# The last token block's closing step of an encoder kernel, with a fixed order on TensorE and its results on three engines

## The chip, the core and the metric

The kernel runs on one core of a Trainium2 chip. The metric is device time in microseconds (us): the median of three executions. One more execution was taken by the hardware profiler; its rows are quoted here. The engines are TensorE (PE, matmuls and transposes), VectorE (DVE), ScalarE (ACT), GpSimd (POOL) and SyncE (SP, which issues the DMAs here). PE reads operands from SBUF and writes PSUM; DVE and ACT read both; POOL adds from SBUF to SBUF here.

## What is computed

One step of a one-layer streaming encoder on 1,024 prompt tokens and 32 sample tokens of width 1,024: a feed-forward part, two attention mixers, and a second feed-forward part. The change lies in the last lines of the layer:

```
h = adaln_in(x, gains[4], sh3, sc3)
x = x + FFN_RES * g3[:, None] * rmsnorm(swiglu(h, w2_gate, w2_up, w2_down), gains[5])

def swiglu(h, w_gate, w_up, w_down):
    return (jax.nn.silu(h @ w_gate) * (h @ w_up)) @ w_down
```

`rmsnorm` divides by the root of the mean square over the 1,024 features (plus a small constant) and multiplies by a gain. All of it is float32.

## The kernel before

Tokens are cut into three blocks of 384, 384 and 288 tokens (`TB`, L27); block 2 holds two tiles of 128 prompt tokens and one of the 32 sample tokens. Inside the kernel an activation is kept with features on the partitions: eight tiles of 128 features (`KT`), tokens along the free dimension. The output wants tokens on the rows, so in the end every 128x128 piece is turned on PE (`te.transpose`).

`ffn` (L525) runs the second feed-forward part in groups of two of the 22 slices of the hidden width. For each block `up` makes gate and up products (48 matmuls each slice in `mm3`, three a product) and `down` multiplies with the down weights into a two-bank PSUM tile `dn` for each pair of feature tiles and adds it into `facc` on DVE (L581), four accumulations a block. In the last group `down` also steps the block's closing step, `finale` (L1297), once after each accumulation, and afterwards leaves it in the list `side`, whose pieces are handed out by `step` between other work and run to the end by `finish` (L488).

`finale` of a block: squares of `facc` on ACT (L364), added up on POOL for the first two pairs of features and on DVE for the others (L368, L370), one matmul set with a vector of ones that sums over the partitions (`pss`, L357; three token tiles, six PE records), a reciprocal root on DVE (L330 to L339, ten small steps on a 128x3 tile), the scaling of `facc` by gate and gain on ACT (L1304) and DVE (L1306) in turn, the turns of `facc` on PE (`py`, L1313: four a piece), and for each piece one DVE instruction (L1315) that multiplies the turned piece by the token's root and adds the residual: `xp <- py * y + xp`. Below, such an instruction is called a result. There are two results to a token tile, and one output DMA to each tile (L1318).

The residual comes from `xs_dram` with features on the partitions as well. `tokens_first` (L1282) loads it (`raw`, L1288), turns it on PE (`px`, L1293) and copies it to `xp` on ACT (L1294). For block 2 it is begun beside the last slice of block 1.

PSUM is held in three pools: `ps2` has two tiles of two banks (`dn`), `ps1` three of one bank (`gate`, `up`, `px`, `py`), `psc` one (`pss`). The order on each engine is made when the kernel is built, by a list scheduler that goes by a model of the times; inside a `manual_schedule` block the named engine keeps the order of the code. In SBUF the tags `u`, `h` and `r` are rings of six, five and three buffers (`xp`; `sq`; `raw`).

Of the kernel before, what the change touches and what calls it, by code (L numbers as in the profile page):

```python
# [7 lines left out]
F32 = mybir.dt.float32  # L8
F32R = mybir.dt.float32r
I32 = mybir.dt.int32  # L10
AF = mybir.ActivationFunctionType
OP = mybir.AluOpType
# [4 lines left out]
D = 1024  # L17
KT = D // 128
DFF = 2816
NF = DFF // 128  # L20
SEQ = 1024
# [5 lines left out]
TB = [(0, 384), (384, 384), (768, 288)]  # L27
SEGS = [[(0, 384, 0)], [(0, 384, 0)], [(0, 256, 0), (256, 288, 1)]]
# [46 lines left out]
def encoder_step(ctx: ExitStack, tc, x_prompt, x_sample, cache_a_k, cache_a_v, cache_b_k, cache_b_v,  # L75
# [27 lines left out]
    def h_tile(shape, name, dt=F32):  # L103
        return hpool.tile(shape, dt, name=name, tag="h")
# [4 lines left out]
    def p2(name, shape=(128, 2, 512)):  # L109
        return ps2.tile(list(shape), F32, name=name, tag="p2")  # L110

    def pc(name, shape=(128, 512)):
        return psc.tile(list(shape), F32, name=name, tag="pc")

    def p1(name, shape=(128, 512)):
        return ps1.tile(list(shape), F32, name=name, tag="p1")
# [225 lines left out]
    def token_cols(w):  # L342
        return [(c, min(128, w - c)) for c in range(0, w, 128)]
# [126 lines left out]
    def token_tiles(tb):  # L470
        t0, w = TB[tb]
        return [(t0 + c, c, 128) for c in range(0, w - w % 128, 128)] + ([(SEQ, w - DEC, DEC)] if w % 128 else [])
# [4 lines left out]
    def step(n):  # L477
        for _ in range(n):
            while side:
                turn[0] += 1  # L480
                i = turn[0] % min(ABREAST, len(side))
                try:
                    next(side[i])
                    break
                except StopIteration:
                    side.pop(i)

    def finish():  # L488
        while side:
            step(1)  # L490
# [3 lines left out]
    def begin(key, gen, first=False):  # L494
        side.insert(0 if first else len(side), marked(key, gen))
# [29 lines left out]
    def ffn(key, H, F, wg, wu, wd, per_group, key_out, after, beside=lambda ff, tb: None):  # L525
        late, pre = [], {}
        plan = rounds(*ROUNDS[key])
        begun = set()
        final = {tb: max(i for i, (g, t) in enumerate(plan) if tb in t) for tb in range(3)}

        def load(r, ff):
            pre[r, ff] = (split_cols(wg, ff), split_cols(wu, ff))

        load(0, 0)
        yield
        for r, (gi, blocks) in enumerate(plan):
            grp = GROUPS[gi]
            wgu, wds, gs = {}, {}, {}

            def up(ff, tb):  # L540
                need((key, tb))
                w = TB[tb][1]
                hi, lo = H[tb]
                ps = [p1("gate"), p1("up")]
                for s in range(2):
                    for k in range(KT):
                        mm3(ps[s][:, :w], wgu[ff][s], k, hi[:, k, :], lo[:, k, :], k == 0, k == KT - 1)
                    step(FAST if gi == 0 else PACE)
                sl = s_tile([128, 384], "sl")
                ae.activation(sl[:, :w], ps[0][:, :w], AF.Silu)  # L550
                ve.tensor_tensor(sl[:, :w], sl[:, :w], ps[1][:, :w], op=OP.mult)  # L551
                g = g_tile([128, 2, 384], "gg", F32R)
                ae.activation(g[:, 0, :w], sl[:, :w], AF.Copy)
                ve.tensor_sub(g[:, 1, :w], sl[:, :w], g[:, 0, :w])  # L554
                gs[ff, tb] = g
                beside(ff, tb)
                if late:
                    late.pop()()

            def down(tb, r=r, grp=grp, wds=wds, gs=gs):  # L560
                w = TB[tb][1]
                new = tb not in begun
                begun.add(tb)
                if new:
                    F[tb] = u_tile(tb, "facc", F32)
                if r == final[tb]:
                    if key_out != "y" or tb == 0:
                        finish()
                    own = marked((key_out, tb), after(tb))
                for mp in range(KT // 2):  # L570
                    ps = p2("dn")
                    for s in range(2):
                        for i, ff in enumerate(grp):
                            g = gs[ff, tb]
                            mm3(ps[:, s, :w], wds[ff], 2 * mp + s, g[:, 0, :w], g[:, 1, :w],
                                i == 0, i == len(grp) - 1)
                    o = F[tb][:, 2 * mp:2 * mp + 2, :]
                    if new:
                        ve.tensor_copy(o, ps[:, :, :w])
                    else:  # L580
                        ve.tensor_tensor(o, ps[:, :, :w], o, op=OP.add)  # L581
                    if r == final[tb]:
                        next(own)
                    step(1)
                if r == final[tb]:
                    side.append(own)

            x, y = grp
            if r:
                load(r, x)  # L590
            load(r, y)
            if r == XAT and key == "h1":
                XIN[1] = load_x(1)
            wgu.update({x: pre[r, x], y: pre[r, y]})
            for ff in grp:
                wds[ff] = split_rows(wd, ff)
            for tb in blocks:
                up(x, tb)
                up(y, tb)
                if len(begun) < 2:  # L600
                    down(tb)
                else:
                    late.append(lambda down=down, tb=tb: down(tb))
            if (gi, 2) == (gi, blocks[-1]):
                per_group(gi)
        late.pop()()


# [669 lines left out]
    F3 = [None] * 3  # L1278

    XP = {}  # L1280

    def tokens_first(tb):  # L1282

        xp = upool.tile([128, 3, KT, 128], F32, name="xp", tag="u", bufs=6)
        for i, (t, c0, n) in enumerate(token_tiles(tb)):
            xt = XP[tb, i] = xp[:, i]
            xr = rpool.tile([128, KT, 128], F32, name="raw", tag="r")
            dma.dma_start(xr[:, :, :n], xs_dram[2][tb][:, :, c0:c0 + n])  # L1288
            yield
            for hf in range(2):  # L1290
                pt = p1("px", (128, 4, 128))
                for k in range(4):
                    te.transpose(pt[:n, k, :], xr[:, 4 * hf + k, :n], ident)  # L1293
                ae.activation(xt[:n, 4 * hf:4 * hf + 4], pt[:n], AF.Copy)  # L1294
                yield

    def finale(tb):  # L1297
# [10 lines left out]
        for i, (t, c0, n) in enumerate(token_tiles(tb)):  # L1308
# [9 lines left out]
            dma.dma_start(dst.rearrange("t (k c) -> t k c", c=128), xt[:n])  # L1318
            yield

    def beside(ff, tb):
        if ff == NF - 1 and tb < 2:
            for t in ((0, 1), (2,))[tb]:
                begin(("xp", t), tokens_first(t))

    for _ in ffn("h3", H3, F3, w2_gate, w2_up, w2_down, lambda gi: None, "y", finale, beside):
        pass
    finish()

# [26 lines left out]
```

## Time and profile before

| | us |
|---|---|
| median of 3 runs | 2213.52 |
| lowest and highest run | 2210.39, 2215.9 |
| profiled execution, own time | 2217.6 |
| its span (first to last instruction) | 2215.8 |
| PE busy | 2161.6 (98%) |
| DVE busy | 1239.1 (56%) |
| ACT busy | 697.8 (31%) |
| POOL busy | 179.2 (8%) |

Times in rows are us from the span's start. A timeline row has start, length, engine, line, operation, output<-inputs, shapes and, in brackets, the idle time before it with what ended it; "x2" merges neighbours. The granted clock is that of PE: 1.00 stands for 2.4 GHz and 0.50 for 1.2 GHz, and a value between is a stretch with some of both.

### The profile page before, as it was taken

To read this page: it belongs to the slowest core of one execution; us is meant where nothing else is said; L and a number is where in the kernel's file an instruction comes from. 1 tells how busy PE (TensorE), PEld (TensorE's weight loads), DVE (VectorE), ACT (ScalarE), POOL (GpSimd) and SP (SyncE) were. 2 spreads that over 40 slices of the span, in tenths; PEclk is the share of its full clock that TensorE was granted. 3 is DMA by queue.
4 is the path that set the end of the run, shared out by engine and by line. 5 is a ranking of instruction groups with operands and counts; after the bars stand their busy time and mean duration, and the time that the engine had idled before them with its cause. 6 is when DMAs were issued, how large, how long until landed. Compare 5 with 4: busy or idle time off the path is not lost.

```text
span 2215.8 us, 33976 instructions
## 1 busy us (share of the span) xinstructions
PE 2161.6 (98%) x14012; PEld 2068.6 (93%) x14012; DVE 1239.1 (56%) x2425; ACT 697.8 (31%) x1450; POOL 179.2 (8%) x281
## 2 busy tenths in 40 slices
PE   6999999999999999899999899999999999999998
PEld 4999999999999999799787589999999999999998
DVE  5788667874333497677444865785333333333336
ACT  4411111111121253576444663542111111111133
POOL 1100000000000023001110313220000000000000
PEclk8999999999999999899999899999999999999999
DMA  9253334434122352111112121424211111111122
GB/s 323 93 153 118 111 96 124 143 101 129 39 66 69 101 184 93 38 39 30 50 30 62 46 77 67 134 86 120 66 58 39 57 39 39 58 38 58 39 69 79
DMA packets 200623, 186.03 MB, mean 84 GB/s; under 512 B 7597, under 2 KB 169813, under 8 KB 199317
## 3 DMA queue, kind: packets, MB, share of 16 engines
q1 hardware_dynamic: 200468, 183.87, 27.1%
q8 instruction: 110, 1.80, 0.3%
q14 instruction: 45, 0.36, 0.1%
HBM read 164.12 MB, written 22.86 MB: 84 GB/s over the span
## 4 chain that ended last, share of the span: by engine, by line
PE 90%; DVE 4%; DMA 3%; ACT 1%; issue 1%; POOL 0%; SPq 0%; ACTq 0%; DVEq 0%; POOLq 0%
PE dn L325 7%; PE dn L326 7%; PE dn L327 7%; PE gate L327 7%; PE gate L326 7%; PE up L327 7%; PE up L326 7%; PE gate L325 7%; PE up L325 7%; PE po L713 3%; PE S L752 2%; PE pq L325 2%; PE pq L327 2%; PE pq L326 2%; DMA raw<-in_w_gate_dram 1%; PE pp L776 1%
## 5 line engine op out<-in xcount | busy, mean ns | idle before, releaser
L326 PE MATMUL gate<-h_lo,w 128*128 128x384 f32 (+1 forms) x1056 | 340.2, 322 | 4.0 <-DVE h_lo L446 4.0
L325 PE MATMUL dn<-gg,w 128*128 128x384 f32 (+1 forms) x1056 | 341.4, 325 | 1.1 <-DVE facc L581 1.0
L581 DVE TENSOR_TENSOR facc<-dn,facc 128x768 f32<-128x768 f32 (+1 forms) x240 | 212.9, 889 | 230.2 <-PE dn L327 229.9
L326 PE MATMUL dn<-gg,w 128*128 128x384 f32 (+1 forms) x1056 | 340.6, 323 | 0.6 <-DVE gg L554 0.6
L325 PE MATMUL gate<-h_hi,w 128*128 128x384 f32 (+1 forms) x1056 | 341.0, 323 | 0.0
L327 PE MATMUL gate<-h_hi,w 128*128 128x384 f32 (+1 forms) x1056 | 340.4, 322 | 0.0
L325 PE MATMUL up<-h_hi,w 128*128 128x384 f32 (+1 forms) x1056 | 340.2, 322 | 0.0
L326 PE MATMUL up<-h_lo,w 128*128 128x384 f32 (+1 forms) x1056 | 340.0, 322 | 0.0
L327 PE MATMUL dn<-gg,w 128*128 128x384 f32 (+1 forms) x1056 | 340.0, 322 | 0.0
L327 PE MATMUL up<-h_hi,w 128*128 128x384 f32 (+1 forms) x1056 | 339.9, 322 | 0.0
L304 DVE TENSOR_TENSOR w<-raw,w 128x1024 fp32r<-128x1024 f32 x187 | 231.5, 1246 | 150.5 <-ACT w L303 150.3
L303 ACT ACTIVATE w<-raw 128x1024 fp32r<-128x1024 f32 x187 | 195.7, 1056 | 266.1 <-PE dn L327 103.5
L550 ACT ACTIVATE sl<-gate 128x384 f32<-128x384 f32 (+1 forms) x132 | 60.9, 462 | 563.9 <-PE gate L327 560.9
L551 DVE TENSOR_TENSOR sl<-sl,up 128x384 f32<-128x384 f32 (+1 forms) x132 | 68.5, 519 | 292.1 <-PE up L327 286.1
L326 PEld LDWEIGHTS gate<-h_lo,w 128*128 128x128 f32 x1056 | 198.6, 188 | 4.6 <-DVE h_lo L446 4.6
L325 PEld LDWEIGHTS dn<-gg,w 128*128 128x128 f32 x1056 | 199.2, 189 | 1.6 <-DVE facc L581 1.2
L326 PEld LDWEIGHTS dn<-gg,w 128*128 128x128 f32 x1056 | 199.2, 189 | 1.0 <-DVE gg L554 0.9
L327 PEld LDWEIGHTS dn<-gg,w 128*128 128x128 f32 x1056 | 199.1, 189 | 0.0
L325 PEld LDWEIGHTS gate<-h_hi,w 128*128 128x128 f32 x1056 | 198.7, 188 | 0.1
L327 PEld LDWEIGHTS gate<-h_hi,w 128*128 128x128 f32 x1056 | 198.7, 188 | 0.0
L327 PEld LDWEIGHTS up<-h_hi,w 128*128 128x128 f32 x1056 | 198.7, 188 | 0.0
L325 PEld LDWEIGHTS up<-h_hi,w 128*128 128x128 f32 x1056 | 198.5, 188 | 0.0
(224 smaller groups left out, 3367.4 us busy)
## 6 DMA issues: line engine op xcount, KB each, us to landing
raw<-in_w_mod_dram SPq DMA_DIRECT2D x56, 512.0 KB, 4.0
raw<-in_w_gate_dram SPq DMA_DIRECT2D x54, 512.0 KB, 4.0
raw<-in_w_up_dram SPq DMA_DIRECT2D x54, 512.0 KB, 4.7
raw<-in_w_down_dram SPq DMA_DIRECT2D x54, 512.0 KB, 4.5
raw<-in_w_in_dram SPq DMA_DIRECT2D x18, 512.0 KB, 4.3
wm<-in_w_mod_dram SPq DMA_DIRECT2D x8, 1024.0 KB, 7.4
raw<-in_w_out_dram SPq DMA_DIRECT2D x13, 512.0 KB, 4.5
xr<-xs SPq DMA_DIRECT2D x16, 384.0 KB, 3.5
```

The source lines that it names most:

```text
L303: ae.activation(w[:, 0], r, AF.Copy)
L304: ve.tensor_sub(w[:, 1], r, w[:, 0])
L325: te.matmul(ps, w[:, 0, k], hi, start=start, stop=False)
L326: te.matmul(ps, w[:, 0, k], lo, start=False, stop=False)
L327: te.matmul(ps, w[:, 1, k], hi, start=False, stop=stop)
L550: ae.activation(sl[:, :w], ps[0][:, :w], AF.Silu)
L551: ve.tensor_tensor(sl[:, :w], sl[:, :w], ps[1][:, :w], op=OP.mult)
L581: ve.tensor_tensor(o, ps[:, :, :w], o, op=OP.add)
L713: te.matmul(po[64 * h:64 * h + 64, :n], vsl(j, h, kn), PT(h, j, kn), start=j == 0, stop=j == nt - 1)
L752: te.matmul(S[:, c:ce], self.T[:, h, :], KQ[:, 0, 128 * k0 + c:128 * k0 + ce], start=True, stop=True)
L776: te.transpose(pp[:, j - j0, :], P[:, 128 * j:128 * j + 128], ident)
```

## The change

`ffn` no longer steps `side` inside the last block's `down`, and it runs `finish` ahead of that `down`, so that what is left of the other blocks' closing steps stands before it in the code. Block 2 gets a closing step of its own, `finale_last`. Its residual is loaded beside its own last slice (`load_xr`) and turned only after the down-projection, in a fixed order on PE. The square sum is taken in three products (the folded sum of three pairs, and both halves of the last pair) instead of one. The results of the 32-token tile are a scaled copy on ACT and an add on POOL; the other four stay on DVE. Each half tile is stored by a DMA of its own.

```diff
-                    step(1)
+                    if key_out != "y" or tb < 2:
+                        step(1)
...
+        if key_out == "y":
+            finish()
         late.pop()()
...
+    def load_xr(tb, i):
+        t, c0, n = token_tiles(tb)[i]
+        xr = XR[tb, i] = rpool.tile([128, KT, 128], F32, name="raw", tag="r")
+        dma.dma_start(xr[:, :, :n], xs_dram[2][tb][:, :, c0:c0 + n])
+
+    def turn_x(xt, xr, n, hf):
+        pt = p1("px", (128, 4, 128))
+        for k in range(4):
+            te.transpose(pt[:n, k, :], xr[:, 4 * hf + k, :n], ident)
+        ae.activation(xt[:n, 4 * hf:4 * hf + 4], pt[:n], AF.Copy)
...
+    def finale_last():
+        f, tb = F3[2], 2
...
+        for c in range(KT // 2):
+            sq = h_tile([128, 2, 384], "sq")
+            ae.activation(sq[:, :, :w], f[:, 2 * c:2 * c + 2, :], AF.Square)
+            if c < 3:
+                e = ge if c < 2 else ve
+                e.tensor_tensor(sq[:, 0, :w], sq[:, 0, :w], sq[:, 1, :w], op=OP.add)
+                if acc is not None:
+                    e.tensor_tensor(sq[:, 0, :w], sq[:, 0, :w], acc[:, 0, :w], op=OP.add)
+                acc = sq
...
+            yield
+
+        def turn_f(pt, i, k0):
+            t, c0, n = toks[i]
+            for k in range(4):
+                te.transpose(pt[:n, k, :], f[:, k0 + k, c0:c0 + n], ident)
+            return pt[:n]
+
+        def residual(i, hf):
+            turn_x(xp[:, i], XR[tb, i], toks[i][2], hf)
+
+        with tc.manual_schedule(engines={mybir.EngineType.PE}):
+            pss = pc("pss")
+            for q, (part, h) in enumerate(((acc, 0), (sq, 0), (sq, 1))):
+                if q == 1:
+                    residual(0, 0)
+                    residual(0, 1)
+                    residual(2, 0)
+                for j, (c0, m) in enumerate(token_cols(w)):
+                    te.matmul(pss[:m, j:j + 1], part[:, h, c0:c0 + m], ones, start=q == 0 and j == 0, stop=q == 2,
+                              skip_group_check=True)
+            y = rstd_cols(pss, w, 1.0 / D)
+            pts = {}
+            for i in (0, 2, 1):
+                bank = p2("py2", (128, 2, 4, 128)) if i < 2 else None
+                for hf in range(2):
+                    if (i, hf) in ((2, 1), (1, 0), (1, 1)):
+                        residual(i, hf)
+                    pts[i, hf] = turn_f(p1("py", (128, 4, 128)) if bank is None else bank[:, hf], i, 4 * hf)
+        for i, hf in ((2, 0), (0, 0), (0, 1), (2, 1), (1, 0), (1, 1)):
+            t, c0, n = toks[i]
+            o, pt, yc = xp[:n, i, 4 * hf:4 * hf + 4], pts[i, hf], y[:n, i:i + 1]
+            if i == 2:
+                z = h_tile([128, 4, 128], "yz")
+                ae.activation(z[:n], pt, AF.Copy, scale=yc)
+                ge.tensor_tensor(o, z[:n], o, op=OP.add)
+            else:
+                ve.scalar_tensor_tensor(o, pt, yc, o, op0=OP.mult, op1=OP.add)
+            dst = y_sample[0] if t == SEQ else y_prompt[0, t:t + 128]
+            dma.dma_start(dst.rearrange("t (k c) -> t k c", c=128)[:, 4 * hf:4 * hf + 4], o)
```

`load_xr` is called for block 2 from `beside`, in the place where `begin(("xp", 2), ...)` was. The scaling of `facc` (L1352 and L1354 of the new code) stands in the lines left out and is as before.

The order on PE from the last down-projection matmuls on, before (`px` turns the residual, `py` the facc; the 28 turns are 24 of block 1 and the first four of block 2):

```order
L327 MATMUL dn<-gg,w 128x288
L1293 MATMUL px<-ident,raw 32x128 x4
L1313 MATMUL py<-ident,facc 128x128 x28
L357 MATMUL pss<-ones,sq 128x1 x2
L357 MATMUL pss<-ones,sq 32x1
L1313 MATMUL py<-ident,facc 128x128 x12
L1313 MATMUL py<-ident,facc 32x128 x8
```

And on PE from the same place in the changed kernel:

```order
L1374 MATMUL pss<-ones,sq 128x1 x2
L1374 MATMUL pss<-ones,sq 32x1
L1295 MATMUL px<-ident,raw 128x128 x8
L1295 MATMUL px<-ident,raw 32x128 x4
L1374 MATMUL pss<-ones,sq 128x1 x2
L1374 MATMUL pss<-ones,sq 32x1
L1374 MATMUL pss<-ones,sq 128x1 x2
L1374 MATMUL pss<-ones,sq 32x1
L1360 MATMUL py_20406<-ident,facc 128x128 x8
L1360 MATMUL py<-ident,facc 32x128 x4
L1295 MATMUL px<-ident,raw 32x128 x4
L1360 MATMUL py<-ident,facc 32x128 x4
```

Behind these come four residual turns, four of `facc`, and the same once more. The 24 turns of block 1 have moved up among the down-projection matmuls (four after the first six of them, then four and four, and twelve ahead of the last twelve matmuls), where 20 residual turns of block 2 stood.

On DVE, from block 2's third and fourth accumulation (L581) on, before (L1306 scales `facc`, L368 and L370 add squares, L1315 are block 1's results):

```order
L581 TENSOR_TENSOR facc<-dn,facc 128x576 x2
L368 TENSOR_TENSOR sq<-sq 128x288
L1306 TENSOR_SCALAR facc<-facc,gcoef 128x256
L1306 TENSOR_SCALAR facc<-facc,gcoef 128x32
L1315 SCALAR_TENSOR_TENSOR xp<-py,ry,xp 128x512
L370 TENSOR_TENSOR sq<-sq 128x288
L1315 SCALAR_TENSOR_TENSOR xp<-py,ry,xp 128x512
L368 TENSOR_TENSOR sq<-sq 128x288
L1306 TENSOR_SCALAR facc<-facc,gcoef 128x256
L1315 SCALAR_TENSOR_TENSOR xp<-py,ry,xp 128x512
```

Behind these rows a scaling step, the last add of squares and three more results stand ahead of the root. And on DVE from the last step of block 1's root on in the changed kernel:

```order
L338 SCALAR_TENSOR_TENSOR ry<-rt,ry 128x3
L1328 SCALAR_TENSOR_TENSOR xp<-py,ry,xp 128x512 x3
L581 TENSOR_TENSOR facc<-dn,facc 128x576
L1354 TENSOR_SCALAR facc<-facc,gcoef 128x256
L1354 TENSOR_SCALAR facc<-facc,gcoef 128x32
L581 TENSOR_TENSOR facc<-dn,facc 128x576
L1328 SCALAR_TENSOR_TENSOR xp<-py,ry,xp 128x512 x3
L1354 TENSOR_SCALAR facc<-facc,gcoef 128x256
L1354 TENSOR_SCALAR facc<-facc,gcoef 128x32
L581 TENSOR_TENSOR facc<-dn,facc 128x576
L1345 TENSOR_TENSOR sq<-sq 128x288
```

Then come a scaling pair, the second add of squares (L1347), a scaling pair and the root. Block 1's six results have moved ahead of the second and the fourth accumulation, and one pair of square adds is gone. On ACT the squares and scalings of block 2 now run without residual copies between them; the copies, two scaled copies (L1389) and the last two residual copies close the queue. On POOL two adds of 32x512 (L1390) follow the adds of squares. SP's order is the old one up to block 1's outputs; then come six half-tile outputs in the order of the tiles 0, 0, 2, 1, 2, 1.

## Rows read from the trace of the kernel before

**Rows 1.** Page: shares of the chain that ended last, by engine.

```profile
PE 90%; DVE 4%; DMA 3%; ACT 1%; issue 1%; POOL 0%; SPq 0%; ACTq 0%; DVEq 0%; POOLq 0%
```

**Rows 2.** Windows: length; busy PE, PEld, DVE, ACT, POOL; clock; DMA share; GB/s.

```profile
2199.00:2206.00 7.00, 5.00 (x40) 4.00 (x38) 6.91 (x16) 3.18 (x7) 0.00 (x0) 1.00 0.27 110
2206.00:2215.80 9.80, 3.75 (x20) 2.47 (x18) 6.23 (x19) 0.00 (x0) 0.00 (x0) 0.61 0.53 202
```

**Rows 3.** Timeline of DVE, from block 2's first accumulation to the end.

```profile
2193.42 0.76 DVE L581 TENSOR_TENSOR facc<-dn,facc 128x576 f32<-128x576 f32 x1 [0.32 <-PE dn L327]
...
2196.72 1.78 DVE L1306 TENSOR_SCALAR facc<-facc,gcoef 128x256 f32<-128x256 f32 x2 [0.65 <-ACT sq L364]
2198.41 1.41 DVE L581 TENSOR_TENSOR facc<-dn,facc 128x576 f32<-128x576 f32 x2
...
2200.29 0.50 DVE L1306 TENSOR_SCALAR facc<-facc,gcoef 128x256 f32<-128x256 f32 x2
2200.69 0.74 DVE L1315 SCALAR_TENSOR_TENSOR xp<-py,ry,xp 128x512 f32<-128x512 f32 x1
...
2204.47 0.46 DVE L370 TENSOR_TENSOR sq<-sq 128x288 f32<-128x288 f32 x1
...
2206.16 0.16 DVE L388 TENSOR_SCALAR rv<-pss 128x2 f32<-128x2 f32 x1
...
2208.36 4.47 DVE L1315 SCALAR_TENSOR_TENSOR xp<-py,ry,xp 128x512 f32<-128x512 f32 x6
```

**Rows 4.** Timeline of SP's queue: the last output DMA.

```profile
2212.86 0.33 SPq L1318 DMA_DIRECT2D out_dram<-xp  x1
```

**Rows 5.** Timeline of PE: the last matmul of the last down-projection.

```profile
2198.61 0.30 PE L327 MATMUL dn<-gg,w 128*128 128x288 f32 x1
```

**Rows 6.** Timeline: adds on POOL, and a DVE accumulation beside one of them.

```profile
2180.69 1.01 POOL L370 TENSOR_TENSOR sq<-sq 128x384 f32<-128x384 f32 x1
2180.75 0.94 DVE L581 TENSOR_TENSOR facc<-dn,facc 128x768 f32<-128x768 f32 x1
...
2196.76 0.81 POOL L368 TENSOR_TENSOR sq<-sq 128x288 f32<-128x288 f32 x1 [0.99 <-ACT sq L364]
```

**Rows 7.** Pieces of the chain: start, length, what, instructions merged.

```profile
2152.27 1.31 PE px L1293 x12
...
2190.56 0.56 PE pss L357 x6
...
2209.26 2.81 PE py L1313 x12
```

**Rows 8.** Timeline of PE: a slow product set, and three long waits.

```profile
26.22 1.44 PE L357 MATMUL pss<-ones,sq 128*128 128x1 f32 x6 [3.20 <-POOL sq L370]
...
920.53 0.39 PE L813 MATMUL Sb<-KSB,qs 128*128 128x256 f32 x1 [2.38 <-ACT Ps L888]
...
1442.92 0.45 PE L326 MATMUL gate<-h_lo,w 128*128 128x384 f32 x1 [2.13 <-DVE h_lo L446]
...
2209.26 2.79 PE L1313 MATMUL py<-ident,facc 128*128 128x128 f32 x12 [2.30 <-DVE xp L1315]
```

**Rows 9.** Windows of PE: length, busy (instructions), granted clock, DMA share, GB/s.

```profile
921.00:921.50 0.50, 0.50 (x5) 0.89 0.07 12
...
924.50:925.00 0.50, 0.50 (x4) 0.70 0.00 0
...
1443.40:1443.80 0.40, 0.40 (x3) 0.79 0.00 0
...
2208.00:2208.50 0.50, 0.00 (x0) 0.72 0.74 295
...
2209.50:2210.00 0.50, 0.50 (x4) 0.50 0.00 0
```

**Rows 10.** Timeline of ACT, one copy; line L467 on POOL: min/median/max ns, shapes.

```profile
2200.54 0.57 ACT L1294 ACTIVATE xp<-px 32x512 f32<-32x512 f32 x1
...
L467 POOL TENSOR_TENSOR facc<-facc,xr x6: 1432/1850/1855, 775.7 to 878.4; 128x768 f32<-128x768 f32 x4, 128x576 f32<-128x576 f32 x2
```

More of the change, by code (lines that the diff above doesn't have):

```diff
@@ L1280, in encoder_step @@
     XP = {}
+    XR = {}
+    def load_xr(tb, i):
[7 more added lines that the diff above has]
+        ae.activation(xt[:n, 4 * hf:4 * hf + 4], pt[:n], AF.Copy)
     def tokens_first(tb):
@@ L1286, in tokens_first @@
             xt = XP[tb, i] = xp[:, i]
-            xr = rpool.tile([128, KT, 128], F32, name="raw", tag="r")
-            dma.dma_start(xr[:, :, :n], xs_dram[2][tb][:, :, c0:c0 + n])
+            load_xr(tb, i)
             yield
+            xr = XR.pop((tb, i))
             for hf in range(2):
[L1291 to L1294, printed above, removed]
+                turn_x(xt, xr, n, hf)
                 yield
@@ L1319, in finale @@
             yield
+    def finale_last():
+        f, tb = F3[2], 2
+        w, toks = TB[tb][1], token_tiles(tb)
+        xp = upool.tile([128, 3, KT, 128], F32, name="xp", tag="u", bufs=6)
+        acc, sq = None, None
+        for c in range(KT // 2):
[7 more added lines that the diff above has]
+                acc = sq
+            for k in (2 * c, 2 * c + 1):
+                for a, b, st in SEGS[tb]:
+                    if k % 2:
+                        ae.activation(f[:, k, a:b], f[:, k, a:b], AF.Copy, scale=gcoef[:, 2, st, k:k + 1])
+                    else:
+                        ve.tensor_scalar(f[:, k, a:b], f[:, k, a:b], gcoef[:, 2, st, k:k + 1], None, op0=OP.mult)
+            yield
[31 more added lines that the diff above has]
+                ge.tensor_tensor(o, z[:n], o, op=OP.add)
+            else:
+                ve.scalar_tensor_tensor(o, pt, yc, o, op0=OP.mult, op1=OP.add)
+            dst = y_sample[0] if t == SEQ else y_prompt[0, t:t + 128]
+            dma.dma_start(dst.rearrange("t (k c) -> t k c", c=128)[:, 4 * hf:4 * hf + 4], o)
@@ L1321, in beside @@
     def beside(ff, tb):
         if ff == NF - 1 and tb < 2:
-            for t in ((0, 1), (2,))[tb]:
-                begin(("xp", t), tokens_first(t))
-    for _ in ffn("h3", H3, F3, w2_gate, w2_up, w2_down, lambda gi: None, "y", finale, beside):
+            if tb == 0:
+                for t in range(2):
+                    begin(("xp", t), tokens_first(t))
+            else:
+                for i in range(3):
+                    load_xr(2, i)
+    for _ in ffn("h3", H3, F3, w2_gate, w2_up, w2_down, lambda gi: None, "y",
+                 lambda tb: finale_last() if tb == 2 else finale(tb), beside):
```

## The prediction

> **What bounds the kernel now.** I began with the page's chain of work that ended last: TensorE (PE) is 90% of the span [rows 1]. So only what PE does or waits for moves the time, and the diff leaves its work alone until the last down-projection. The rest of this text is about the last 25 us. There I read two windows: from 2199 to 2206 PE is busy for 5.0 of 7.0 us and VectorE (DVE) for 6.9; from 2206 on PE has 3.8 of 9.8, at a mean granted clock of 0.61 [rows 2]. The closing step is therefore a DVE chain with PE as its servant. The timeline of DVE gives its stations: the first accumulation of block 2 at 2193.42, the last ending at 2199.82, the last add of squares at 2204.47, six results of block 1 squeezed between and behind these (the first at 2200.69), the start of the reciprocal root at 2206.16, six results of block 2 from 2208.36 to 2212.83 [rows 3]. The last output transfer is issued at 2212.86 and the span ends 2.94 us later [rows 4].
>
> **The change part by part.** All times are on the axis of the profiled execution, whose time is 2217.6 us, 1.8 above its span. The median of the three runs is 2213.52, so I work out a difference and add it to the median.
>
> *Block 1's finale moves ahead of block 2's down-projection.* Its last six results leave the end of DVE's queue and now stand, three and three, before the second and the fourth accumulation. They need block 1's reciprocal root, whose last step follows the first accumulation as before. So DVE's queue from 2193.42 to the folded sum of squares is a plain sum of starts from the rows of DVE: four accumulations at 0.67 (two take 1.41 together, so the next starts 0.07 before one of 0.74 ends), one small step 0.2, six results at 0.67 by the same overlap (one runs 0.74; 4.0), three scaling pairs at 0.40 (the pair from 2200.29 is followed at 2200.69), and the two adds of squares, about 0.4 each. That is 2.7 + 0.2 + 4.0 + 1.2 + 0.8 = 8.9, so the folded sum is ready at 2202.3 [rows 3]. PE, with 24 turns of block 1 among the down-projection instead of 20 residual turns, ends it some 0.5 us later than the 2198.9 of before, at about 2199.4 [rows 5], ahead of the accumulations that wait for it. ScalarE's squares are ready earlier than the adds. One cost goes: in the present order two scaling pairs fell under GpSimd's adds of squares; the one at 2196.72, beside two adds in a row from 2196.76, took 1.78 us against 0.50 alone [rows 3, 6]. In the new order they stand behind three results each, when GpSimd has no add running. That is inside the 8.9.
>
> *Block 2's residual turns move behind the down-projection and after the first of three square-sum products.* Here is the price. PE finishes at 2199.4, and its next instruction in the fixed order is the product that wants the folded sum of 2202.3. It waits 2.9 us, with everything queued behind it: twelve turns, two more products, and DVE's root that wants the last. Behind the wait stand 6 + 12 + 12 records (a product set is six records, a row block of turns four). At the full clock a set costs 0.56 and twelve turns 1.31, so 0.56 + 1.31 + 1.12 = 3.0. At the half clock a set takes 1.4 (the 26.22 row) and twelve turns 2.81 (that row holds short waits, so it is an upper value), so 1.4 + 2.8 + 2.8 = 7.0 [rows 7, 8].
>
> Which clock? A wait that long after dense work took the clock down in each place where I looked. PE stood 2.38 us until 920.53; the grant fell in the window at 921.0 and came back in that at 924.5. It stood 2.13 until 1442.92 and the grant fell in the window at 1443.4. At the end of this kernel it stood 2.30 until 2209.26; the grant fell in the window at 2208.0 and was 0.50, that is 1.2 GHz instead of 2.4, for the turns that followed [rows 8, 9]. So I take PE to be at the half clock for about the first 4.1 us after it resumes, as from 920.53 to the window at 924.5. In these pass the first set (1.4) and the turns (2.7 of 2.8); the two last sets run at the full clock: 1.4 + 2.8 + 1.1 = 5.3. The Trainium skill, "TensorE: Matmul & The Clock Gate", section "Why this matters for your kernels", warns against gaps between bursts of matmuls, which speaks against this order; these rows agree with it.
>
> The products thus end at 2202.3 + 5.3 + 0.1 = 2207.7, and the first result starts a root later (2206.16 to 2208.36, 2.20, with four hundredths for the signal): 2209.9, against 2208.36 before. So the product stage costs 1.5 us.
>
> *The results themselves.* Before, six on DVE take 4.47 and the end follows 2.97 later, 7.44 from first start to span end [rows 3, 4]. In the new order DVE has four. The two of the 32-token tile become a scaled copy on ScalarE (0.57, by the 32x512 copy) and an add on GpSimd. No row has GpSimd at 512 columns; 384 take 1.01 and 288 take 0.81, so by the slope 512 take 1.3; below I would put 1.0 (the 384 row), above 1.85, the median of 768 columns (L467's four of them) [rows 6, 10]. I take 1.3. From the first result's start: first copy to 0.57, first add 0.64 to 1.93, second add to 3.3, its transfer issued by 3.65. DVE's last pair waits for two residual turns whose buffers come free with those copies: freed at 0.57, turn to 1.2, copy to 1.8, then the result to 2.6; the next turn, copy and result end at 3.5. SP issues in order and the second add stands before the last result there, so the last transfer starts at 3.7 and the span ends at 6.6, which saves 0.8. With GpSimd at 1.0 DVE's 3.5 sets the end (saves 1.0); at 1.85 the adds end at 4.35 and the gain is lost (costs 0.3). Three halves more to issue at 0.33 [rows 4] lie under waits. The new residual loads cost nothing: they keep their place on SP's queue, ahead of the outputs, and their data is wanted only at 2203. If they were late, PE would wait longer at the first turn.
>
> *Does GpSimd hold DVE here?* The scaling pair beside GpSimd's adds stretched to 1.78 [rows 3, 6]; an accumulation, with one operand from PSUM, took 0.94 beside a GpSimd add of 1.01, its usual time [rows 6]. The results have that second form, so I put nothing on it. The Trainium skill, "SBUF — State Buffer", section "Who interferes with whom", would say the same of a DVE instruction with at most one SBUF input, and the sum by it is the one below. By the scaling row instead, a result could wait out an add, which would add up to 1.3 us and make the sum 2.0 instead of 0.7.
>
> Sum: 1.5 - 0.8 = +0.7 us. Profiled 2218.3, median 2213.52 + 0.7 = **2214.2**.
>
> **The rivals.**
> *The clock holds, or is back at once.* Then 3.0 replaces 5.3: -2.3 + 0.7 = -1.6 us, 2211.9. For it: from 2199 to 2206 PE stood for 2.0 us in several short pieces and the grant stayed at 1.00 [rows 2]. Against it: every single wait above 2 us that I read. It also needs the 2.9 us to be much shorter, that is an earlier folded sum.
> *Slower: the clock stays low to the end.* The tail of this kernel did not get it back by 2209.5, nor in the mean of 0.61 to the end [rows 2, 9]. It decides if the clock is not full by about 2207. Then the products end at 2202.3 + 7.0 + 0.1 = 2209.4, and PE has 36 turns left (8 + 7 x 4), at 2.81 per twelve 8.4, so that PE and not DVE sets the last result: 2217.8, a result of 0.75, 2.97 to the end, 2221.5. That is +5.7 us, 2219.2. For it: that tail itself, the nearest row in place and kind of work. Against: from 920.53 PE worked on without gaps and the clock came back, and behind the new wait it has no gap either.
> *GpSimd sets the end.* At 1.85 an add, or with DVE held, +1.8 to +2.0, 2215.4. Against: the slope of two sizes.
> *It doesn't do what it says*: the compiled order on each engine shows the turns behind the down-projection and the results on three engines, so only the size is open.
>
> **How the numbers follow.** The forecast (half clock for some 4 us) has 0.6, the clock that holds 0.15, the clock low to the end 0.15, GpSimd 0.1. The three runs of before span 2210.39 to 2215.9, 2.7 either way, which a median of three takes down to about 1.5. The range goes from the clock that holds less such a spread, 2210, to just under the slow rival, 2218.5; left out are half of the slow rival, and runs beyond. A measurement of this kernel can tell 0.3% from no change, that is 6.6 us. No case reaches it: the slow rival with the upper scatter gives 0.04 for slower, something unseen 0.02 for faster, 0.94 for the same.
>
> **What would show it.** Step one: DVE's folded sum ends at 2202.3 and PE stands from 2199.4 to then; if it stands under 1.5 us, the queue sum is wrong. Step two: the granted clock falls to 0.50 near 2201 to 2203 and the twelve turns take 2.5 to 2.8 us; at 1.3 the clock rival holds. Step three: root start to first result 2.2, first result to span end 6.6. If PE's turns and not the copies end the last waits of DVE, the slow rival is true. The prediction is wrong if the change reaches anything before 2190, or if GpSimd's adds take over 1.5 us.

## The result, and the profile after

The changed kernel takes 2218.64 us, the median of 20 executions (2214.25 to 2225.28), beside 2214.43 (2210.39 to 2218.48) for the kernel before: a ratio of 1.0018 with a 95% interval of 1.001 to 1.0025. On the median that the prediction started from, 2213.52, that is 2217.5, or +4.0 us where +0.7 was forecast (the two medians of this measurement stand 4.2 apart). It lies inside the range and within the 0.3% that count as no change, but the interval leaves 1 out. A second measurement of the same kernel, in another job, gave 1.0 (0.9991 to 1.0009). The two intervals do not overlap, and why is the main question below.

The profiled execution after took 2219.39 us with a span of 2217.6 (before 2217.6 and 2215.8). The page's chain by engine, after:

```profile
PE 87%; DVE 5%; DMA 4%; ACT 1%; issue 1%; POOL 0%; SPq 0%; DVEq 0%; ACTq 0%; POOLq 0%
```

Against [rows 1] PE has lost three points and DVE has won one. The timeline of PE, from the last down-projection matmul on (to be held against [rows 5, 7, 8]):

```profile
2198.19 0.29 PE L327 MATMUL dn<-gg,w 128*128 128x288 f32 x1
2201.56 0.73 PE L1374 MATMUL pss<-ones,sq 128*128 128x1 f32 x6 [3.07 <-ACT facc L1352]
2202.22 1.85 PE L1295 MATMUL px<-ident,raw 128*128 128x128 f32 x12
2203.86 2.18 PE L1374 MATMUL pss<-ones,sq 128*128 128x1 f32 x12
2205.97 2.83 PE L1360 MATMUL py<-ident,facc 128*128 128x128 f32 x12
2208.59 1.06 PE L1295 MATMUL px<-ident,raw 128*32 128x128 f32 x4
...
2211.69 0.60 PE L1360 MATMUL py<-ident,facc 128*128 128x128 f32 x4
```

PE stands 3.07 us in front of the first product. (The releaser named is ACT's; the folded sum of the next fence ended at the same moment, 2201.41.) Nothing is idle between the rows behind it: from there on PE itself is the chain. The timeline of DVE in the same stretch, which answers to [rows 3]:

```profile
2192.56 0.76 DVE L581 TENSOR_TENSOR facc<-dn,facc 128x576 f32<-128x576 f32 x1 [0.49 <-PE dn L327]
...
2199.11 0.50 DVE L1354 TENSOR_SCALAR facc<-facc,gcoef 128x256 f32<-128x256 f32 x2
...
2200.96 0.45 DVE L1347 TENSOR_TENSOR sq<-sq 128x288 f32<-128x288 f32 x1
...
2206.08 0.16 DVE L388 TENSOR_SCALAR rv<-pss 128x2 f32<-128x2 f32 x1 [4.25 <-PE pss L1374]
...
2208.40 1.41 DVE L1392 SCALAR_TENSOR_TENSOR xp<-py,ry,xp 128x512 f32<-128x512 f32 x2
2212.40 1.41 DVE L1392 SCALAR_TENSOR_TENSOR xp<-py,ry,xp 128x512 f32<-128x512 f32 x2 [2.59 <-PE py L1360]
```

DVE waits 4.25 us for the products and 2.59 us for PE's last turns; before, no more than 0.11 us lay between the six results that [rows 3] show as one row. Windows of PE (length, busy, granted clock, DMA share, GB/s), to be held against [rows 9]:

```profile
2202.50:2203.00 0.50, 0.50 (x7) 1.00 0.00 0
2203.00:2203.50 0.50, 0.50 (x6) 0.78 0.00 0
2203.50:2204.00 0.50, 0.50 (x5) 0.50 0.00 0
...
2209.50:2210.00 0.50, 0.50 (x4) 0.50 0.00 0
2210.00:2210.50 0.50, 0.50 (x5) 0.89 0.99 369
```

The grant held through the wait and for 1.7 us of work behind it, then fell to 1.2 GHz and stayed there until 2210. GpSimd's two adds, and the last output DMA in SP's queue (for [rows 4, 10]):

```profile
2210.92 2.49 POOL L1390 TENSOR_TENSOR xp<-yz,xp 32x512 f32<-32x512 f32 x2 [12.22 <-ACT yz L1389]
```

```profile
2214.09 0.38 SPq L1394 DMA_DIRECT2D out_dram<-xp  x1
```

### The profile page after: what moved, and what is told of

Same layout as the page of the kernel before. It is cut to its first block, busy times and chain, and to the rows that moved or that the text cites. A ratio compares the mean times of both kernels' runs of the same rounds, so it can differ in the third digit from the quotient of the medians.

```text
span 2217.6 us, 34009 instructions
## 1 busy us (share of the span) xinstructions
PE 2161.4 (97%) x14024; PEld 2070.4 (93%) x14024; DVE 1235.0 (56%) x2421; ACT 698.7 (32%) x1452; POOL 181.7 (8%) x283
## 4 chain that ended last, share of the span: by engine, by line
PE 87%; DVE 5%; DMA 4%; ACT 1%; issue 1%; POOL 0%; SPq 0%; DVEq 0%; ACTq 0%; POOLq 0%
PE dn L325 7%; PE up L326 7%; PE up L327 7%; PE up L325 7%; PE dn L326 7%; PE gate L327 7%; PE dn L327 7%; PE gate L326 7%; PE gate L325 7%; PE po L716 3%; PE S L755 2%; PE pq L325 2%; PE pq L327 2%; PE pq L326 2%; DMA raw<-in_w_up_dram 1%; DMA raw<-in_w_gate_dram 1%
## 5 line engine op out<-in xcount | busy, mean ns | idle before, releaser
L581 DVE TENSOR_TENSOR facc<-dn,facc 128x768 f32<-128x768 f32 (+1 forms) x240 | 212.9, 889 | 229.3 <-PE dn L327 229.0
L327 PEld LDWEIGHTS up<-h_hi,w 128*128 128x128 f32 x1056 | 199.0, 188 | 0.0
L326 PEld LDWEIGHTS up<-h_lo,w 128*128 128x128 f32 x1056 | 198.6, 188 | 0.0
```

The source lines that it names most:

```text
L326: te.matmul(ps, w[:, 0, k], lo, start=False, stop=False)
L327: te.matmul(ps, w[:, 1, k], hi, start=False, stop=stop)
```

## The experiments

The start of block 2's first accumulation moves by several us between executions (2187.88 to 2195.36 in the profiles here), for reasons ahead of the change. So I measure the **tail**: from that start (2193.42 before, 2192.56 after) to the end of the span. In the table all times count from there. "Low" is where the windows show the half clock, to about half a microsecond (held: no fall before PE's last instruction); "root" is the start of L388. Each ratio is to the kernel before in the same job.

| run | PE's wait | low | root | first result | tail | ratio, 95% interval |
|---|---|---|---|---|---|---|
| before | - | 15 to end | 12.74 | 14.94 | 22.38 | |
| before_again | - | held | 12.74 | 14.94 | 21.91 | |
| after | 3.07 | 10.5-17.5 | 13.52 | 15.84 | 25.04 | 1.0018, 1.001-1.0025 |
| again | 3.07 | held | 12.41 | 14.73 | 22.35 | 1.0, 0.9991-1.0009 |
| again2 | 3.08 | 8-18 | 14.95 | 17.27 | 26.47 | |
| fill24 | 0.46 | held | 12.41 | 14.73 | 22.29 | 0.9996, 0.9985-1.0006 |
| resid_first | 1.70 | 11-14 | 11.19 | 13.49 | 21.82 | 1.0002, 0.9992-1.0012 |
| nofinish | 4.34 | 11-21 | 15.68 | 18.00 | 27.83 | 1.0021, 1.0011-1.0031 |
| all_first | 0.26 | 11.5-15 | 11.09 | 13.39 | 20.76 | 0.9998, 0.9989-1.0007 |
| all_first_b | 0.25 | 11.5-15 | 11.08 | 13.38 | 20.74 | 0.9997, 0.9987-1.0006 |
| res_dve | 3.08 | 8.5-18.5 | 14.94 | 17.76 | 26.17 | 1.0021, 1.001-1.0032 |
| fold | 4.22 | 11-14.5 | 10.91 | 14.98 | 23.22 | 1.0009, 1.0-1.0017 |
| five | 0 | 11-18 | 12.42 | 14.72 | 22.94 | 1.0003, 0.9994-1.0011 |
| all_first_fold | 1.75 | 11.5-15 | 11.18 | 13.47 | 20.85 | 0.9996, 0.9986-1.0006 |

**The same two kernels again (again, again2, before_again).** No edit.

> The changed kernel once more, for a second profile. The tail is counted from the start of block 2's first accumulation to the span's end: 22.4 us before (2193.42 to 2215.8), 25.0 in the changed kernel (2192.56 to 2217.6). Theory C (clock): the price is what TensorE's granted clock loses after the 3.07 us wait for the folded sum; when it falls and comes back differs from execution to execution, so the tail here may be anything from 23 to 27 us, and what differs is seen in the turns and products behind the wait. Theory D (order): the price is the work that now stands behind that wait, whatever the clock; the tail is 25.0 within 0.3.

> The changed kernel a third time, one look. In the two profiles so far the grant fell 1.7 us after the wait (tail 25.0) and did not fall (tail 22.4), with the same order and the same wait of 3.07 us. C: the tail is 22.4 where the grant holds, and longer by about half of the time at 0.50 in which TensorE is what is waited for.

> The kernel before, profiled once more. If the tail's length is a matter of the order alone, the tail from block 2's first accumulation to the span's end is 22.4 within 0.2, as in the first profile. If the granted clock of the end differs between executions of one kernel here too, it lies between 20.9 (clock held, as much as the twelve turns gain at the full clock, 1.5) and 26, and the windows of PE show it.

Of `again`, the timeline of PE and DVE, and two windows of PE:

```profile
2199.55 0.73 PE L1374 MATMUL pss<-ones,sq 128*128 128x1 f32 x6 [3.07 <-ACT facc L1352]
2200.21 1.53 PE L1295 MATMUL px<-ident,raw 128*128 128x128 f32 x12
2201.58 1.34 PE L1374 MATMUL pss<-ones,sq 128*128 128x1 f32 x12
2202.86 1.53 PE L1360 MATMUL py<-ident,facc 128*128 128x128 f32 x12
...
2202.96 0.16 DVE L388 TENSOR_SCALAR rv<-pss 128x2 f32<-128x2 f32 x1 [3.14 <-PE pss L1374]
...
2207.57 1.41 DVE L1392 SCALAR_TENSOR_TENSOR xp<-py,ry,xp 128x512 f32<-128x512 f32 x2 [0.87 <-PE py L1360]
```

```profile
2203.00:2203.50 0.50, 0.50 (x6) 1.00 0.00 0
...
2209.00:2209.50 0.50, 0.00 (x0) 1.00 0.59 221
```

The order and the wait are those of the fences above to a hundredth, and the grant never falls before PE's work is done. Twelve turns of `facc` take 1.53 us, not 2.83. In `again2` the wait is again the same, and the grant falls inside it:

```profile
2200.00:2200.50 0.50, 0.00 (x0) 0.64 1.01 410
...
2210.00:2210.50 0.50, 0.50 (x5) 0.62 0.00 0
```

```profile
2201.24 1.18 PE L1374 MATMUL pss<-ones,sq 128*128 128x1 f32 x6 [3.08 <-ACT facc L1352]
2202.34 2.82 PE L1295 MATMUL px<-ident,raw 128*128 128x128 f32 x12
```

So one program gave tails of 22.35, 25.04 and 26.47, and the theory that the order alone sets the tail (25.0 within 0.3) falls. Between `again` and after, the stage from first product to root takes 3.41 against 4.52 us, and first to last result 3.70 against 5.41: 2.8 together, where the tails differ by 2.7. Program, order and the wait of 3.07 us are the same and the clock differs: that it makes the difference is shown; why the grant falls in one execution and not in another is not. (The Trainium skill, "TensorE: Matmul & The Clock Gate", section "What's actually happening", says that the gate's window of activity runs freely, not tied to the kernel, so the moment of a change differs between executions; no run here shows the window, and the three profiles agree with a moment that the code does not fix.)

The kernel before varies too, but less. In `before_again` the clock holds to the end and its six results take 4.03 us, against 4.47 in [rows 3]; its last turns:

```profile
2203.43 4.03 DVE L1315 SCALAR_TENSOR_TENSOR xp<-py,ry,xp 128x512 f32<-128x512 f32 x6
```

```profile
2204.33 1.84 PE L1313 MATMUL py<-ident,facc 128*128 128x128 f32 x12 [2.30 <-DVE xp L1315]
```

Its wait of 2.30 is the one of [rows 8], where the clock fell. Nor is it only the end: the wait of 2.13 of [rows 8], behind which the grant fell, leaves it at 1.00 here:

```profile
1439.56 0.44 PE L326 MATMUL gate<-h_lo,w 128*128 128x384 f32 x1 [2.13 <-DVE h_lo L446]
```

```profile
1440.00:1440.50 0.50, 0.50 (x5) 1.00 0.00 0
```

One profile each way: before costs 0.47 us more with the clock down, the new order 2.7 to 4.1 more. With the clock up in both, the new tail is 0.44 longer.

Why do the two ratios of the result differ? The mean granted clock of the whole program is on record for every execution of the changed kernel. From the first job to the second the mean time of the changed kernel fell from 2218.63 to 2216.08 us and its mean clock rose from 0.9855 to 0.9865; the mean time of the kernel before rose from 2214.67 to 2215.75. Inside each job time follows the clock (correlation -0.94), with 1.45 us for each thousandth. So the clock goes with some 1.5 of the 2.55 us. The rest, and the 1.1 us of the kernel before, stay open, and as this clock covers the whole program, it does not show that the falls lie in the tail.

**Fill the wait (fill24).** Turns of `ident` into a tile of their own keep PE at work while it would wait.

```diff
+            filler = p2("fill", (128, 4, 128))
+            for _ in range(24):
+                te.transpose(filler[:, 0, :], ident, ident)
             for q, (part, h) in enumerate(((acc, 0), (sq, 0), (sq, 1))):
```

> The changed kernel with 24 more turns of the identity matrix on TensorE, into a PSUM tile of their own that nobody reads, between the last down-projection matmul and the first square-sum product: they fill 2.6 of the 3.07 us in which TensorE stood. C: the grant stays at 1.00, the first product, twelve turns and two products take 3.0 instead of 4.4 us, the turns of facc behind them 3.9 instead of 6.3, so that the first result comes 1.4 earlier and the last about 3.3 earlier: tail 21.7, within 0.7. D: no change, 25.0 or more.

```profile
2196.07 2.78 PE L1370 MATMUL fill<-ident 128*128 128x128 f32 x24
2199.31 0.73 PE L1377 MATMUL pss<-ones,sq 128*128 128x1 f32 x6 [0.46 <-ACT facc L1352]
```

The clock held, the tail (22.29) lies in the 21.7 within 0.7 expected for that, and the stations are those of `again` within 0.06 us. So at a held clock PE's wait in itself costs nothing; what costs is the work that stands behind it. Whether the filler keeps the clock up is open, since `again` held it with no filler, and the two ratios overlap.

**Put the work into the wait (resid_first, all_first).** `resid_first` turns the three half tiles of the gap ahead of the first product; `all_first` turns all six there, and none among the turns of `facc`.

```diff
             pss = pc("pss")
+            for i in (0, 2, 1):
+                residual(i, 0)
+                residual(i, 1)
             for q, (part, h) in enumerate(((acc, 0), (sq, 0), (sq, 1))):
-                if q == 1:
-                    residual(0, 0)
-                    residual(0, 1)
-                    residual(2, 0)
...
-                    if (i, hf) in ((2, 1), (1, 0), (1, 1)):
-                        residual(i, hf)
```

> The changed kernel with the three residual half tiles (twelve turns) ahead of the first square-sum product instead of behind it: they run while TensorE stood. C: they take 1.3 at the full clock, the wait left is 1.7 us, and a grant that holds gives a tail of 21.0 to 22.0; if the 1.7 us still take the clock down, 23 to 24. D: only the turns' 1.6 us leave the path, tail 23.4.

> The changed kernel with all six residual half tiles (24 turns, 2.6 us at the full clock) ahead of the first square-sum product, so that useful turns fill nearly all of TensorE's wait and none stands behind the products or among the turns of facc. C (clock): the wait left is under 0.6 us, the grant holds at 1.00 in every execution, and the tail (start of block 2's first accumulation to span end; before 22.4, changed 25.0 and 22.4 in two profiles) is 20.0, within 0.7: folded sum at 9.0, three products 1.9, root 2.3, results and adds 3.3, last transfer 3.5. D (order): the turns' places alone are worth at most 1.6 plus 1.0, tail 20 to 21 whatever the clock; the two differ in the grant.

> The same kernel as all_first, once more. If 20.76 us of tail is the order's, with the clock down for 3.5 us, a profile with the clock held gives 20.0 to 20.5 and one with it down longer up to 22; the medians of both executions taken together stand 1.0 to 2.0 us below the kernel before, a ratio of 0.9993 to 0.9998. If the first median of 2212.92 was scatter, this one lies within 0.5 us of the kernel before.

The timeline of PE and DVE in `all_first`, then two of its windows:

```profile
2194.91 2.89 PE L1295 MATMUL px<-ident,raw 128*128 128x128 f32 x24
2198.06 2.13 PE L1373 MATMUL pss<-ones,sq 128*128 128x1 f32 x18 [0.26 <-DVE sq L1347]
2200.12 4.51 PE L1360 MATMUL py<-ident,facc 128*128 128x128 f32 x24
...
2200.23 0.16 DVE L388 TENSOR_SCALAR rv<-pss 128x2 f32<-128x2 f32 x1 [1.56 <-PE pss L1373]
...
2204.74 1.41 DVE L1389 SCALAR_TENSOR_TENSOR xp<-py,ry,xp 128x512 f32<-128x512 f32 x2 [0.80 <-PE py L1360]
```

```profile
2200.00:2200.50 0.50, 0.50 (x6) 1.00 0.00 0
2201.00:2201.50 0.50, 0.50 (x5) 0.50 0.00 0
```

The root starts 1.3 us earlier than in `again` (11.09 against 12.41), which is the twelve turns (1.37 us between the starts there) taken out of the path. The grant still fell, with a wait of 0.26 and PE at work on both sides of it, but only 24 turns were left to slow, and half of their time lies beside the root. The tail is 20.76 and 20.74 in two profiles, just above the 20.0 within 0.7 that I expected with a grant held in every execution; it fell in both. The other theory's 20 to 21, whatever the clock, is what came: here the places of the turns count for more than the clock. `resid_first`, with the clock down for some 3 us, has 21.82, which is what a held clock was to give it: the fall cost less than I had put. Both tails are shorter than either of before. In time the gain is not settled: medians of 2212.92 and 2213.49 beside 2214.31 and 2214.77, 1.3 to 1.4 lower, near what the tails would have (1.2 to 1.6); but the ratios of 0.9998 and 0.9997 are worth only 0.4 to 0.7 us, and both intervals hold 1.

**Block 1's finale left where it was (nofinish).**

```diff
-        if key_out == "y":
-            finish()
         late.pop()()
```

> The changed kernel without the finish ahead of the last down-projection: block 1's remaining turns and results stand behind it in the code, and the scheduler puts eight of the turns behind the last down-projection matmul. Its six results still stand ahead of the folded sum on VectorE. C: TensorE's wait becomes some 2.2 us, long enough for the clock to fall as it did in waits of 2.1 to 2.4 us; tail 25.0 within 1. D: the same queue of VectorE, tail 25.0 within 0.5. Both hold that block 1's place by itself costs nothing; a tail near 22.4 would say that it is the price.

The timelines of PE, DVE and POOL show why the wait grew to 4.34 us:

```profile
2203.84 0.73 PE L1372 MATMUL pss<-ones,sq 128*128 128x1 f32 x6 [4.34 <-DVE sq L1345]
```

```profile
2197.08 1.36 DVE L1352 TENSOR_SCALAR facc<-facc,gcoef 128x256 f32<-128x256 f32 x2
...
2203.24 0.45 DVE L1345 TENSOR_TENSOR sq<-sq 128x288 f32<-128x288 f32 x1
```

```profile
2196.71 0.81 POOL L1343 TENSOR_TENSOR sq<-sq 128x288 f32<-128x288 f32 x1 [0.77 <-ACT sq L1340]
2197.59 0.80 POOL L1345 TENSOR_TENSOR sq<-sq 128x288 f32<-128x288 f32 x1
```

A scaling pair falls beside GpSimd's adds again and takes 1.36 instead of 0.50, as in [rows 3, 6]; the folded sum ends 10.1 us after the first accumulation instead of 8.9. Both theories expected a tail of 25, within 1 or 0.5; it was 27.83, with the low clock lasting 10 us, so neither had this right. The early `finish` is worth 1.3 us of the folded sum by itself, 0.9 of it in that pair.

**All results on DVE (res_dve).**

```diff
-            if i == 2:
+            if False:
```

> The changed kernel with all six results on VectorE again (no scaled copy on ScalarE, no add on GpSimd, the half-tile stores kept). If sharing the results over three engines gains what the forecast put on it, this tail is longer by 0.5 to 1 us than the changed kernel's at the same clock (22.4 where the grant holds, 25.0 where it falls); if TensorE's turns set the last results, the tail is the same within 0.3.

```profile
2210.49 2.71 DVE L1392 SCALAR_TENSOR_TENSOR xp<-py,ry,xp 32x512 f32<-32x512 f32 x4 [0.64 <-PE py L1360]
2213.99 1.41 DVE L1392 SCALAR_TENSOR_TENSOR xp<-py,ry,xp 128x512 f32<-128x512 f32 x2 [0.79 <-PE py L1360]
```

And DVE's last pair in `again2`:

```profile
2213.38 1.41 DVE L1392 SCALAR_TENSOR_TENSOR xp<-py,ry,xp 128x512 f32<-128x512 f32 x2 [2.47 <-PE py L1360]
```

The low stretch of `res_dve` is close to that of `again2`, and so is its root (14.94 and 14.95), which makes the two a pair. The tails are 26.17 and 26.47: with the clock down, three engines gain nothing over one, since DVE's last pair waits for PE in both. No profile of `res_dve` has the clock held, so for that case it is not shown.

**How many products (fold, five, all_first_fold).** `fold` adds the last pair on DVE as well and takes one product, with the three half tiles behind it. `five` starts from `all_first`, drops DVE's adds of squares and takes five products. `all_first_fold` is `all_first` with the single product of `fold`.

```diff
-            if c < 3:
+            if c < 4:
                 e = ge if c < 2 else ve
...
-            for q, (part, h) in enumerate(((acc, 0), (sq, 0), (sq, 1))):
+            for q, (part, h) in enumerate(((acc, 0),)):
```

```diff
-            if c < 3:
-                e = ge if c < 2 else ve
+            parts += [(sq, 0), (sq, 1)]
+            if c < 2:
+                e = ge
...
-            for q, (part, h) in enumerate(((acc, 0), (sq, 0), (sq, 1))):
+            for q, (part, h) in enumerate([(acc, 0)] + parts[4:]):
```

> The changed kernel with one square-sum product instead of three: the last pair is added up on VectorE too (0.45 + 0.4 us more there), and twelve records of TensorE and, with the twelve residual turns now behind the product, these turns too leave the root's path. Same clock assumed: tail 20.6 where the grant holds (folded sum at 9.85, product 0.6, root 2.3, then as in the changed kernel 7.8 from first result to end), some 2 us more where it falls. The wait in front of the product grows to 3.9 us, so theory C wants the grant to fall here in most executions.

> Edit on top of the all-residuals-first order: the two adds of squares on DVE (0.4 each in its queue) go; PE takes both halves of the third and of the fourth pair as products of their own, five sets instead of three (two more sets, 1.1 us at the full clock, of which all but the last pair's can run before the last square is there). Theory that DVE's queue up to the folded sum sets the start of the root: from block 2's first accumulation the root starts 0.4 to 0.8 us earlier, the tail (first accumulation to span end) is 20.0 to 20.4 at the full clock instead of the 20.76 measured with the clock down for 3.5 us, and the median stays 1.5 to 2.5 us below that of the kernel before. Theory that PE and its clock set it: the two added sets stand on the path, 1.1 at the full clock and 2.8 at the half, the tail is 21.5 to 23 and the median equals that of the kernel before within 1 us.

> All six residual half tiles ahead of the products, and one product of the fully folded sum (the last pair's add of squares on DVE too). From the run that folded without moving all residuals the folded sum came 10.15 us after block 2's first accumulation and the root started 0.76 later. Theory that DVE's queue sets the start of the root: root starts at 10.9 after the first accumulation (11.1 with three products), PE waits about 1.4 us in front of the product, tail 19.9 to 20.3 with the clock held, 20.5 to 21.5 with it down; median 1.5 to 2.5 us below that of the kernel before. Theory that PE's own stream sets it (24 turns and then the product): the root starts at 9.3 to 9.6, the wait is gone.

In `fold` the root starts earliest of all (10.91), and nothing is won: the turns that stood between the products now stand between the root and the first result, which waits for PE. The tail of 23.22, with the clock down for 3.5 us, is 0.6 more than I had put for that case.

```profile
2204.66 1.41 DVE L1391 SCALAR_TENSOR_TENSOR xp<-py,ry,xp 128x512 f32<-128x512 f32 x2 [1.89 <-PE py L1360]
```

In `five` PE has no wait behind the down-projection, and the grant falls all the same:

```profile
2201.12 2.89 PE L1295 MATMUL px<-ident,raw 128*128 128x128 f32 x24
2203.85 3.90 PE L1374 MATMUL pss<-ones,sq 128*128 128x1 f32 x30
2207.68 5.38 PE L1361 MATMUL py<-ident,facc 128*128 128x128 f32 x24
```

```profile
2206.00:2206.50 0.50, 0.50 (x6) 0.80 0.00 0
2207.00:2207.50 0.50, 0.50 (x4) 0.50 0.00 0
```

The theory that DVE's queue sets the root falls for this order: with 24 turns and five sets in a row PE's own stream does (root at 12.42, tail 22.94, in the 21.5 to 23 of the other theory). In `all_first_fold` it holds in part: PE waits 1.75 us for the folded sum, but the root comes at 11.18, not at the 10.9 expected. One set behind a later sum is worth the same as three sets behind an earlier one, and the tail (20.85) is that of `all_first`; no gain in time can be told (median 2215.89 beside 2214.77, ratio 0.9996).

## Why the prediction was right and wrong, step by step

- *Folded sum 8.9 us after the first accumulation, PE standing 2.9.* Right: 8.85 (2192.56 to 2201.41) and 3.07. With it stand the moves in the queue: scaling pairs of 0.50 where one had 1.78 [rows 3], and residual turns that never waited for their loads.
- *"A wait that long took the clock down in each place where I looked."* This step failed. The same wait of 3.07 to 3.08 was followed by a fall 1.7 us after PE resumed, by none, and by one inside the wait; and the grant fell behind waits of 0.26 and of nothing. The three places of [rows 8, 9] were of one execution, and that was too little for a rule: in the trace of before every wait of PE above 2 us behind its start has a fall in it or within 1 us behind it, while in `before_again` the same waits of 2.13 and 2.30 have none. The low stretch was forecast at 4.1 us from the moment of resuming; it was 6.8, nothing and 10.
- *Products 5.3 us.* With the signal that is 5.4 to the root; it took 4.52, 3.41 and 5.94 in the three profiles. The forecast's two bounds, 3.0 and 7.0, hold all three. The upper one was too high: in `again2`, with the clock down through the whole stage, a set took 1.1 and twelve turns 2.6, not the 1.4 and 2.8 read from [rows 8]. What the forecast did not price: where the clock fell, it was still down in the next stage (to 17.5 and 18 in the table, with first results at 15.84 and 17.27).
- *Root 2.2.* It took 2.32.
- *First result to span end 6.6, a saving of 0.8.* Mis-sized most: 9.2, 7.62 and 9.2. Two terms of it failed. The last result was to end 3.5 behind the first: 3.70 at the full clock, but 5.41 and 5.29 with it down, since PE's turns and not the copies ended DVE's last wait, which the prediction had named as the mark of its slow rival. (It is no mark: in `again`, with the clock held, DVE's last pair waits 0.87 us for PE too.) And the end was to follow 3.1 us behind the last result; it follows 3.5 to 3.9 in the new kernels (3.8 after), against 2.94 and 2.97 in the two profiles of before. Of that, the last issue starts 0.28 behind the result, since SP is still issuing the one ahead, and the span ends 3.5 behind that issue instead of 2.94 [rows 4]. The last transfer is now half a tile of 128 tokens, 256 KB, where it was the 128 KB tile; that this is the cause of the 0.6 is argued, not tested. In windows of a quarter of a microsecond the DMA engines stop moving data 1.3 to 1.4 us behind the last issue in the two profiles of before and 1.6 to 1.7 in after and `again`, so the moving of data is about half of the 0.6; the other half lies behind it and is open. These 0.9 us eat the forecast saving of 0.8 at any clock.
- *GpSimd's add 1.3, the accumulation form not held by it.* Right: two in 2.49, and a pair of results beside them at their usual 1.41. The adds end at 2213.41, DVE's last result at 2213.81, so GpSimd does not set the end.
- *The sum.* The queue moved forward as forecast: the folded sum came at 8.85, before at 11.51 (2204.93) [rows 3]. At the full clock the root gained only 0.33 of these 2.66 us (12.41 against 12.74): the rest went into twelve turns and three product sets behind the wait, where one set stood before. The root then takes 0.12 more and the end 0.65 more (7.62 against 6.97): +0.44 with the clock up in both. The rival of the held clock had put -1.6 against the first profile (22.38), where `again` (22.35) stands at 0: its products were 0.3 too short, its end 1.0, and wait and root 0.1 each. With the clock down, the profiles stand 2.7 and 4.1 above the first one of before: the slow rival had the mechanism, and its +5.7 the price too high, since the grant came back before the last turns. The forecast's half-way clock, 0.6 of the chance, was in no profile. That 2217.5 lies in the range is owed to its width, which reached to just under the slow rival, and not to the +0.7: this sum rests on a clock that no profile shows and on a saving at the end that was a cost. The measured +4.0 and 0 go in part with the granted clock of the two jobs (0.9855 and 0.9865), and for the rest are open.

## What to carry to other kernels

A fixed order that puts work behind a waiting instruction lengthens the path by that work, and by nearly twice as much at the half clock (twelve turns took 1.53 us in `again` and 2.82 in `again2`): put work that depends on nothing into the wait, as the residual turns here. Where a stage is a chain of short PE pieces, price it at both clocks and profile the same kernel more than once before a difference of a few us is put down to the code. A stage that is shared among more engines gains nothing while one engine still ends the last wait; look which transfer is last, and how large it is.

## What the hardware did that I had not expected

- One program, one order, waits equal to a hundredth: the grant held to the end, fell 1.7 us behind a 3.07 us wait, or fell inside it, and the tail went from 22.35 to 26.47 us.
- A wait is not needed: in `five` the grant fell at 2206.3 with PE at work since the down-projection, among one-column products; in `all_first` and `all_first_b` it fell at the same station, about 0.6 us after the root's start, in both profiles. Whether turns and one-column products are too little work to hold the clock is not tested: `again` held it through 11 us of them and the wait (2196.5 to 2207.5), and no run has other work in their place.
- The first accumulation of block 2 started anywhere from 2187.88 to 2195.36 us, 7.5 us apart, in kernels that differ only behind it or a few us ahead. The longest and the shortest tail differ by 7.1, so times of single executions say little about this change.
